# A hybrid decoder layer on one core: attention dealt in units of 128 keys, the first norm put ahead, the last tile cut in two

## The chip, the cores and the metric

The kernel runs on one core of one Trainium2 chip. The metric is device time in microseconds (us), the median of three runs. The engines are TensorE (PE: matrix products and transposes; its weight loads are listed apart as PEld), VectorE (DVE), ScalarE (ACT), GpSimd (POOL) and SyncE (SP, which issues most transfers). Each works through its own instructions in the order fixed when the program is built, and waits on semaphores for the others.

## The reference

One decoder layer over 512 tokens with 1024 channels, in float32:

```
u = rms_norm(x, norm_pre_mix);  proj = u @ w_in      # 9 projections
y_a = hgrn2_mixer(...)                               # gated recurrence, 8 heads
y_b = nsa_mixer(...)                                 # attention, 16 heads of 64, 4 groups of keys
merged = sigmoid(ga) * (y_a @ w_branch_a) + sigmoid(gb) * (y_b @ w_branch_b)
h = x + rms_norm(merged @ w_out, norm_post_mix)
v = rms_norm(h, norm_pre_mlp)
h = h + rms_norm(square(relu(v @ w_up)) @ w_down, norm_post_mlp)
e = (p @ w_ple) * sigmoid(h @ w_ple_gate)
out = h + rms_norm(e, norm_ple)
```

`nsa_mixer` has three branches for each head: softmax over 31 compressed keys, over selected blocks and over a window. With 512 tokens there are only 8 blocks of 64, all of them selected, and the window spans all earlier keys, so that the second and third branch are both full causal attention, each with keys and values of its own. Each branch is scaled by a gate and the three are added.

## The kernel before

Every product is made from three passes: each operand is split into a high part and a remainder, and high by high, high by remainder and remainder by high are added up in PSUM. A weight chunk is loaded by SP into `raw`; ACT casts it to `whi`, DVE subtracts for `wlo` (`pair_of`, `split`, lines 58 to 60 and 105 to 110). During attention the remainder is formed by ACT and an adding transfer from POOL's queue instead (`split_by_transfer`, lines 62 to 65).

**Start.** Token tile 0 is normed: ACT squares and sums, DVE and POOL form the factor, DVE writes `un` in two halves (L198), PE transposes them, ACT and DVE split the result into `uh` and `ul`. The first two weight chunks are cast and split on the same two engines at the same time.

**Attention** (`attend`) handles one group of four heads at a time, g = 0 to 3, over four query tiles t and two branches br: eight steps (t, br), each with t + 1 key tiles of 128. `scores` makes the scores of one step (PE, L474 and L476), their maxima (DVE, L478), the exponentials (ACT, L482), the scaling by gate and sum (DVE L492, ACT L495). `values` goes over the key tiles: PE transposes four heads (L162), ACT and DVE split them into `pth` and `ptl` (L59, L60), PE multiplies by V (L505, L506). Scores are made one step ahead. A generator yields after each step. So there are 20 key tiles in each group and 80 in all.

**The main stream** is the work that needs none of this: the projections for later groups (`kv_job`, `q_main`, each 96 products of 256 columns) and for the gates (`gate_tanh`, 24 products of 512 columns each). `mark` notes an instruction of attention with a weight, `rec` notes the first product of each threesome in the main stream, and `spread` then ties each of these, by an order-only dependency, behind the mark that lies in the same proportion. The order within an engine is otherwise made by a planner that takes what is ready by its own costs, earlier program text first. In the text before, whole steps of two groups are advanced (`advance`, lines 601 to 606), then a stretch of main stream is written, then `spread` is called; the transposes of queries and keys (`tr_r`, `q_rest`, `cmp_probs`) come in one lump for a group. Those transposes and the main stream share two PSUM banks (`mainp`, tag `main`). Keys and queries wait for their transposes in one tile, `stage`, with one buffer.

After attention come the recurrence (`hgrn_main`, `hgrn_head`), the two branch products, `w_out`, the MLP and the last product, `w_ple_gate`: two column halves by four token tiles, each half tile 24 products of 512 columns, then `evac_e` (lines 1179 to 1194): tanh, multiply, square with sum, the factor (`rms`), two final multiply-adds, two transfers by SP.

Of the kernel before, what the change touches and what calls it, by code (L numbers as in the profile page):

```python
# [7 lines left out]
FT = mybir.dt.float32  # L8
# [10 lines left out]
D = 1024  # L19
# [9 lines left out]
def hybrid_layer(ctx: ExitStack, tc: tile.TileContext, x, p, w_in, w_branch_a, w_branch_b, w_out,  # L29
# [40 lines left out]

    def mark(m, w=1.0):
        marks.append((m.ins, w + (marks[-1][1] if marks else 0.0)))
# [31 lines left out]

    def pair_of(src, a, b):
# [66 lines left out]
    with tc.tile_pool(name="pre", reuse_waits="tile", bufs=2) as pre, \  # L172
# [16 lines left out]
        for t in range(NT):  # L189
# [6 lines left out]
            for g in range(2):  # L196
                c = slice(g * 512, g * 512 + 512)
                dve.scalar_tensor_tensor(un[:, c], xs[t][:, c], rs, wps[:, c], op0=OP.mult, op1=OP.mult)  # L198
# [149 lines left out]
    def kv_job(pr, ck, cv, kdst, vdst, chunks=None):  # L348
        KH, KL, V = [], [], vdst
        st = ns.tile([128, 2, NT, 2, 128], FR, name="stage", bufs=1)  # L350
# [16 lines left out]
        for j in range(2):  # L367
            for src, dst, e in ((hn, KH, 0), (ln, KL, 1)):
                ps = tr_r([src[:, t, j] for t in range(NT)])
                kt = kdst[2 * j + e]  # L370
                if e:
                    act.copy(kt, ps.bitcast(FT))
                else:
                    dve.tensor_copy(kt, ps)
                dst.append(kt)
        return KH, KL, V

    def q_job(g):
        return q_rest(*q_main(g))

    def q_main(g):
        qsn = ns.tile([128, NT, 4, 128], FR, name="stage", bufs=1)
# [19 lines left out]
    def q_rest(qsn, qn):  # L402
        qs = [ns.tile([128, 512], FR, name="qs", tag="qs", bufs=8) for _ in range(4)]
# [6 lines left out]
        qt = []  # L410
# [8 lines left out]
        return qs, qt  # L419

    def cmp_soft(g, qt):
# [6 lines left out]
        sc = ns.tile([128, NT, 4, 32], FT, name="sc")  # L428
# [16 lines left out]
    def cmp_probs(sc):  # L445
        chl = []
# [10 lines left out]
        return chl  # L457

    def attend(g, qs, chl, kvs):
# [38 lines left out]
        def values(t, br, Ps, py):  # L498
            V = kvs[br][2]
            for kt in range(t + 1):  # L500
# [5 lines left out]
                mark(pe.matmul(py, V[j][:, kt], lo, start=False, stop=False), 1.0)  # L506

        def store(t, py):
# [27 lines left out]
    def together(*gens):  # L536
        live = list(gens)
        while live:
            live = [g for g in live if next(g, None) is not None]
# [8 lines left out]
    kv_dst = [kv_tiles(ns)]  # L548

# [4 lines left out]
    k0 = kv(0, 0, first_chunks)  # L554
# [24 lines left out]
    k1 = kv(0, 1)  # L579
    ph = cmp_core(0, kcd)  # L580
    q0, qt0 = q_job(0)
# [5 lines left out]
    c0 = cmp_probs(sc0)  # L587
# [13 lines left out]
    def advance(a, na, b=None, nb=0):  # L601
        for i in range(max(na, nb)):
            if i < na:
                next(a, None)
            if i < nb:
                next(b, None)

    a0 = attend(0, q0, c0, (k0, k1))
    advance(a0, 7)
    kb = kv(1, 0)  # L610
    gate_tanh(C_GB, gB_d, gp, 3, 4)
    q1 = q_main(1)
    spread(.9)
    marks.clear()
    rec.clear()
    gate_tanh(C_GB, gB_d, gp, 4, 5)
    q1, qt1 = q_rest(*q1)
    spread(1)
    c1 = cmp_probs(cmp_soft(1, qt1))
    spread(1)  # L620
    a1 = attend(1, q1, c1, (k0, k1))
    advance(a0, 3, a1, 6)
    kb = kb, kv(1, 1)
    q2 = q_main(2)
    spread(1)
    marks.clear()
    rec.clear()
    gate_tanh(C_GB, gB_d, gp, 5, 6)
    q2, qt2 = q_rest(*q2)
    spread(1)  # L630
    c2 = cmp_probs(cmp_soft(2, qt2))
    spread(1)
    a2 = attend(2, q2, c2, kb)
    advance(a1, 4, a2, 7)
    gate_tanh(C_GB, gB_d, gp, 6, 7)
    q3 = q_main(3)
    spread(.8)
    marks.clear()
    rec.clear()
    gate_tanh(C_GB, gB_d, gp, 7, 8)  # L640
    q3, qt3 = q_rest(*q3)
    spread(1)
    c3 = cmp_probs(cmp_soft(3, qt3))
    spread(1)
    a3 = attend(3, q3, c3, kb)
    advance(a2, 3, a3, 5)
    gate_tanh(C_GA, gA_d, gp, 0, 1)
    spread(1.1)
    advance(a3, 5)
    gate_tanh(C_GA, gA_d, gp, 1, 2)  # L650
    gate_tanh(C_GA, gA_d, gp, 2, 3)
    spread(1)
# [274 lines left out]
    def rows_of(ch, stat, nk, c, t, evac):  # L927
        ps = tp.tile([128, 512], FT, name="acc", tag="acc", bufs=3)
        s = slice(t * 128, t * 128 + 128)
        for k in range(nk):  # L930
            hi, lo = ch[k // 2]
            pe.matmul(ps, stat[0][:, k, s], hi[:, k % 2], start=(k == 0), stop=False)  # L932
            pe.matmul(ps, stat[0][:, k, s], lo[:, k % 2], start=False, stop=False)  # L933
            pe.matmul(ps, stat[1][:, k, s], hi[:, k % 2], start=False, stop=(k == nk - 1))  # L934
# [15 lines left out]
    def rms(pl, ss, eps):  # L950
        a = pl.tile([128, 1], FT, name="rsa")
        b = pl.tile([128, 1], FT, name="rsb")
        r = pl.tile([128, 1], FT, name="rsr")
        dve.tensor_scalar(a, ss[:, 0:1], 1.0 / D, eps, op0=OP.mult, op1=OP.add)
        dve.scalar_tensor_tensor(b, ss[:, 1:2], 1.0 / D, a, op0=OP.mult, op1=OP.add)
# [108 lines left out]
    def up_group(g):  # L1064
# [28 lines left out]
        if g == 1:  # L1093

            tc.add_manual_dep(m.ins, formed[-1].ins.name, mybir.DependencyInfo(
                mybir.DependencyClass.NoSync, mybir.DependencyReason.DATA), reason="forms first")
# [77 lines left out]
    sse = [ff.tile([128, 2], FT, name="sse", bufs=4) for _ in range(NT)]  # L1174
# [4 lines left out]
    def evac_e(c, t, ps):  # L1179
        tg = tgs[:, t % 2]  # L1180
        act.activation(tg, ps, AF.Tanh, scale=0.5)
        d = pw[:, t, c * 512:c * 512 + 512]
        dve.scalar_tensor_tensor(d, tg, 1.0, d, op0=OP.add, op1=OP.mult)
        sumsq(ff, d, sse[t][:, c:c + 1])
        z = rest[:, 2 * (t % 2) + c]
        if c == 0:
            z = d
        dve.tensor_mul(z, d, halves(w_pl)[c])
        if c == 1:
            r = rms(ff, sse[t], 4 * EPS)  # L1190
            for i, zz in enumerate((pw[:, t, 0:512], z)):
                o = rest[:, 2 * (t % 2) + i]
                dve.scalar_tensor_tensor(o, zz, r, halves(facc[:, t])[i], op0=OP.mult, op1=OP.add)
                sp.dma_start(out[t * 128:(t + 1) * 128, i * 512:i * 512 + 512], o)
    proj_n(w_ple_gate, (vh2, vl2), NK, evac_e)
# [57 lines left out]
```

## Time and profile before

| | us |
|---|---|
| median of 3 runs (lowest, highest) | 1234.18 (1232.11, 1237.09) |
| the profiled execution | 1235.09 |
| its span, first to last instruction | 1233.1 |
| PE busy in the span | 1191.1 |
| PE weight loads (overlapping) | 1039.4 |
| DVE busy | 781.4 |
| ACT busy | 641.3 |
| POOL busy | 146.8 |

The profiled execution lies 0.9 us above the median and 2.0 us above its own span. Busy time is the share of time in which an engine has an instruction in flight; since products are pipelined, a busy PE is not a PE at its best rate. The mean granted TensorE clock is 0.994 of full.

### The profile page before, as it was taken

The numbers are of one execution on the slowest core, as the hardware profiler recorded it, in microseconds if no ns is written. First come the engines' busy times: TensorE is split into PE (matmuls) and PEld (weight loads), VectorE is DVE, ScalarE is ACT, GpSimd is POOL, SyncE is SP. The second block draws the span as 40 slices with busy tenths as digits, with TensorE's granted clock in tenths as the row PEclk, the third lists the DMA queues.
The fourth block names the chain that finished last, engine by engine and source line by source line (L and its number), as shares of the span: only waits on it lengthen the run. The fifth ranks groups of instructions, "written<-read, shape, count | busy, mean of one in ns | idle before, by whom it ended". The sixth has DMA issues, their size and how long they took to land.

```text
span 1233.1 us, 18788 instructions
## 1 busy us (share of the span) xinstructions
PE 1191.1 (97%) x7159; PEld 1039.4 (84%) x7159; DVE 781.4 (63%) x1407; ACT 641.3 (52%) x1291; POOL 146.8 (12%) x282
## 2 busy tenths in 40 slices
PE   7999899999999999999999999999999999999997
PEld 6888797787878889898978788888989889889885
DVE  6774667737787366767675454588527457554664
ACT  6555878757886433434343322366637427336442
POOL 2020232221311110101010201000000000000000
PEclk9999999999999999999999999999999999999999
DMA  6337534242522432222223895434413324227401
GB/s 179 103 106 181 132 81 105 57 109 58 120 60 78 137 103 61 77 64 74 67 72 91 236 229 167 162 132 150 141 35 127 114 69 143 80 69 245 153 13 69
DMA packets 134188, 137.07 MB, mean 111 GB/s; under 512 B 8865, under 2 KB 108113, under 8 KB 134098
## 3 DMA queue, kind: packets, MB, share of 16 engines
q1 hardware_dynamic: 120352, 107.49, 30.0%
q0 software_dynamic: 5792, 19.93, 7.2%
q10 hardware_dynamic: 7954, 8.46, 2.1%
q8 instruction: 56, 0.92, 0.3%
q14 instruction: 34, 0.28, 0.1%
HBM read 111.73 MB, written 14.68 MB: 103 GB/s over the span
## 4 chain that ended last, share of the span: by engine, by line
PE 68%; DVE 2%; ACT 1%; DMA 1%; issue 0%; POOL 0%; ACTq 0%; DVEq 0%; POOLq 0%; SPq 0%
PE up L1054 11%; PE ps L86 6%; PE ps L87 6%; PE ps L88 5%; PE acc L1141 5%; PE acc L1140 5%; PE acc L1142 5%; PE lev L726 3%; PE acc L932 3%; PE acc L934 3%; PE acc L933 3%; PE ps L137 2%; PE ps L139 2%; PE ps L138 2%; PE tr L1054 2%; PE tr L162 1%
## 5 line engine op out<-in xcount | busy, mean ns | idle before, releaser
L59 ACT CAST whi<-raw 128x1024 fp32r<-128x1024 f32 (+1 forms) x181 | 188.4, 1046 | 215.3 <-PE acc L1142 59.1
L60 DVE TENSOR_TENSOR wlo<-raw,whi 128x1024 fp32r<-128x1024 f32 (+1 forms) x181 | 221.6, 1229 | 117.8 <-ACT whi L59 112.5
L137 PE MATMUL ps<-whi,uh 128*128 128x256 f32 (+1 forms) x512 | 147.4, 289 | 3.7 <-ACT gt L212 2.3
L138 PE MATMUL ps<-wlo,uh 128*128 128x256 f32 (+1 forms) x512 | 146.4, 286 | 0.2 <-DVE wlo L60 0.2
L139 PE MATMUL ps<-whi,ul 128*128 128x256 f32 (+1 forms) x512 | 146.3, 286 | 0.0
L86 PE MATMUL ps<-uh,whi 128*128 128x512 f32 x288 | 117.9, 409 | 0.2 <-DVE chl L456 0.2
L88 PE MATMUL ps<-uh,wlo 128*128 128x512 f32 x288 | 114.6, 398 | 0.3 <-DVE wlo L60 0.3
L87 PE MATMUL ps<-ul,whi 128*128 128x512 f32 x288 | 114.8, 399 | 0.0
L137 PEld LDWEIGHTS ps<-whi,uh 128*128 128x128 f32 x512 | 96.6, 189 | 6.8 <-ACT gt L212 2.9
L1141 PE MATMUL acc<-wlo,fh 128*128 128x512 f32 x256 | 101.2, 395 | 0.0
L1140 PE MATMUL acc<-whi,fh 128*128 128x512 f32 x256 | 100.5, 395 | 0.0
L1142 PE MATMUL acc<-whi,fl 128*128 128x512 f32 x256 | 99.9, 395 | 0.0
L138 PEld LDWEIGHTS ps<-wlo,uh 128*128 128x128 f32 x512 | 96.8, 189 | 1.2 <-DVE wlo L60 0.5
L139 PEld LDWEIGHTS ps<-whi,ul 128*128 128x128 f32 x512 | 96.7, 189 | 0.5 <-DVE ul L60 0.2
L482 ACT ACTIVATE P<-ps_s,nm 128x128 f32<-128x128 f32 (+3 forms) x128 | 67.7, 538 | 15.3 <-DVE nm L478 12.5
L478 DVE TENSOR_REDUCE nm<-ps_s 128x1 f32<-128x384 f32 (+3 forms) x88 | 55.7, 635 | 29.0 <-PE ps_s L476 28.5
L60 DVE TENSOR_TENSOR ptl<-tr,pth 128x512 fp32r<-128x512 f32 x82 | 55.6, 685 | 21.9 <-ACT pth L59 21.2
L88 PEld LDWEIGHTS ps<-uh,wlo 128*128 128x128 f32 x288 | 54.1, 188 | 12.5 <-DVE wlo L60 0.4
L474 PE MATMUL ps_s<-kt,qs 128*128 128x128 f32 (+3 forms) x256 | 60.4, 339 | 4.2 <-ACT P L482 3.7
L86 PEld LDWEIGHTS ps<-uh,whi 128*128 128x128 f32 x288 | 54.1, 188 | 11.1 <-PE py L532 0.6
L87 PEld LDWEIGHTS ps<-ul,whi 128*128 128x128 f32 x288 | 54.2, 188 | 10.3
L59 ACT CAST pth<-tr 128x512 fp32r<-128x512 f32 x82 | 47.7, 594 | 26.9 <-PE tr L162 25.9
(323 smaller groups left out, 2916.2 us busy)
## 6 DMA issues: line engine op xcount, KB each, us to landing
raw<-in_w_in_dram SPq DMA_DIRECT2D x58, 512.0 KB, 3.9
raw<-in_w_up_dram SPq DMA_DIRECT2D x32, 512.0 KB, 3.7
raw<-in_w_down_dram SPq DMA_DIRECT2D x32, 512.0 KB, 4.3
wlo<-raw POOLq DMA_DIRECT2D x18, 512.0 KB, 4.8
raw<-in_w_in_dram SPq DMA_DIRECT2D x17, 256.0 KB, 3.4
raw<-in_w_branch_a_dram SPq DMA_DIRECT2D x8, 512.0 KB, 8.6
raw<-in_w_branch_b_dram SPq DMA_DIRECT2D x32, 128.0 KB, 6.2
raw<-in_w_out_dram SPq DMA_DIRECT2D x8, 512.0 KB, 4.5
```

What stands on the lines that cost most here:

```text
L59: act.copy(hi, src)
L60: return dve.tensor_sub(lo, src, hi)
L86: rec.append(pe.matmul(ps, lh, rh, start=first, stop=False).ins)
L87: pe.matmul(ps, lh, rl, start=False, stop=False)
L88: pe.matmul(ps, ll, rh, start=False, stop=last)
L137: rec.append(pe.matmul(o, stat[0][:, k, s], hi[:, i], start=(k == 0), stop=False).ins)
L138: pe.matmul(o, stat[0][:, k, s], lo[:, i], start=False, stop=False)
L139: pe.matmul(o, stat[1][:, k, s], hi[:, i], start=False, stop=(k == NK - 1))
L1054: pe.matmul(ps[:, c], l[:, k, cs], r[:, k], start=f and n == 0, stop=e and n == 2, skip_group_check=True)
L1140: pe.matmul(ps, fh[:, k % 4, s], hi[:, k % 2], start=(k == 0), stop=False)
L1141: pe.matmul(ps, fh[:, k % 4, s], lo[:, k % 2], start=False, stop=False)
L1142: pe.matmul(ps, fl[:, k % 4, s], hi[:, k % 2], start=False, stop=(k == NK - 1))
```

## The change

- The low parts of the first weight chunks are ordered, on DVE, behind the second half of the norm of token tile 0 (`behind`, `lows`).
- `attend` yields after each key tile instead of after each step: a unit of 128 keys. `units` advances a group by n units and behind each takes one piece from another generator: `queries` (4 + 2 transposes of queries, the compressed scores, 4 transposes of probabilities) or `keys` (4 transposes of keys).
- The order of the stage is written anew. Each group has 20 units: nine, beside the next group's `q_main` (for the last group two gate tiles); then eleven, beside one gate tile and a `kv` job (groups 0 and 1) or two gate tiles (groups 2 and 3). `spread(1)` is called at each seam. The next group's first scores are written ahead of the last three units, except from group 1 to group 2, where they are written behind the last `kv` job and its key transposes. The number of products, transposes and gate tiles is the same.
- `stage` gets two buffers; `sc` has one instead of two; the tile `yl` is gone, its values are written over `ytmp`.
- At the end, the last token tile's second column half is computed as two pieces of 256 columns, with the sum of squares in three parts for that tile; in all four tiles the transfers of the second half are issued by ACT instead of SP.

The diff, cut to its core:

```
+    def behind(m, first, why):
+        tc.add_manual_dep(m.ins, first.ins.name, ... NoSync ..., reason=why)
...
-        w_split[0](hi, lo, src)
+        lows.append(w_split[0](hi, lo, src))
...
+                if t == 0 and g == 1:
+                    for low in lows:
+                        behind(low, m, "norm first")
...
-        st = ns.tile([128, 2, NT, 2, 128], FR, name="stage", bufs=1)
+        st = ns.tile([128, 2, NT, 2, 128], FR, name="stage", bufs=STAGES)    # 2
...
+        def keys():
+            for j in range(2):
+                for src, dst, e in ((hn, KH, 0), (ln, KL, 1)):
+                    ps = tr_r([src[:, t, j] for t in range(NT)])
...
+                    yield True
+        return (KH, KL, V), keys()
...
+    def queries(g, qm, qs, chl):
+        qt = []
+        yield from q_rest(*qm, qs, qt)
+        sc = cmp_soft(g, qt)
+        yield True
+        yield from cmp_probs(sc, chl)
...
-            yl = at.tile([128, 512], FR, name="yl", bufs=1)
+            yl = tmp.bitcast(FR)
...
-            values(t, br, pend, py)
+            units = values(t, br, pend, py)
             pend = nxt
-            if br:
-                pe.matmul(py, vch[:, t % 2, g], chl[t // 2], start=False, stop=True)
-                store(t, py)
-            yield True
+            for kt in range(t + 1):
+                next(units)
+                if br and kt == t:
+                    pe.matmul(py, vch[:, t % 2, g], chl[t // 2], start=False, stop=True)
+                    store(t, py)
+                yield True
...
+    def units(a, n, pieces=iter(())):
+        for _ in range(n):
+            next(a)
+            next(pieces, None)
+    a = attend(0, q0, c0, (k0, k1))
+    next(a)
+    left, kb = iter(()), []
+    for g in range(4):
+        units(a, 9, left)
+        whole(left)
+        if g < 3:
+            qm = q_main(g + 1)
+        else:
+            gate_tiles(2)
+        spread(1)
+        if g == 3:
+            units(a, 11)
+            gate_tiles(2)
+            spread(1)
+            break
+        qs, chl = [], []
+        pieces = queries(g + 1, qm, qs, chl)
+        units(a, 8, pieces)
+        kvs = (k0, k1) if g == 0 else kb
+        nxt = attend(g + 1, qs, chl, kvs)
+        if g != 1:
+            next(nxt)
+        units(a, 3, pieces)
+        whole(pieces)
+        gate_tiles(1 if g < 2 else 2)
+        if g < 2:
+            k, left = kv(1, g)
+            kb.append(k)
+        spread(1)
+        if g == 1:
+            whole(left)
+            next(nxt)
+        a = nxt
...
+            (act if o else sp).dma_start(out[t * 128:(t + 1) * 128, o:o + n], oo)
...
+            cuts = (0, 256, 512) if c and t == NT - 1 else (0, 512)
+            for n0, n1 in zip(cuts, cuts[1:]):
+                rows_of(ch, (vh2, vl2), NK, c, t, lambda ...: evac_e(c, t, ps, n0, n1), n0, n1)
```

## Rows read from the trace of the kernel before

**Rows 1.** The page: busy us, share of the span, instructions.

```profile
PE 1191.1 (97%) x7159; PEld 1039.4 (84%) x7159; DVE 781.4 (63%) x1407; ACT 641.3 (52%) x1291; POOL 146.8 (12%) x282
```

**Rows 2.** Windows: from:to, length, busy us by engine, granted clock, DMA share, GB/s.

```profile
133.00:410.00 277.00, 261.49 (x1656) 221.74 (x1655) 198.63 (x432) 208.14 (x527) 66.49 (x118) 0.99 0.36 84
240.00:265.00 25.00, 21.10 (x148) 18.69 (x145) 10.72 (x24) 15.08 (x33) 8.88 (x22) 0.93 0.48 104
277.00:291.00 14.00, 10.96 (x60) 8.21 (x59) 13.32 (x31) 10.56 (x28) 1.91 (x2) 0.88 0.40 95
291.00:324.00 33.00, 33.00 (x227) 30.16 (x225) 20.58 (x46) 26.16 (x66) 10.84 (x20) 1.00 0.31 68
324.00:360.00 36.00, 34.00 (x207) 27.35 (x205) 30.58 (x68) 30.40 (x81) 5.50 (x10) 1.00 0.42 100
```

**Rows 3.** PE's groups by shape, 133 to 410 us; first and last of 21.

```profile
L162 PE MATMUL tr<-ident,P 128*128 128x128 f32 x320 | 54.2, 280 | 2.8 <-DVE P L492 2.3 <-ACT P L495 0.3
...
L505 PE MATMUL py<-pth,V 128*128 128x512 f32 x80 | 34.6, 433 | 3.9 <-ACT pth L59 3.9
...
L476 PE MATMUL ps_s<-causal,identr 128*128 128x512 f32 x8 | 3.6, 444 | 0.0
```

**Rows 4.** The chain of waits: start, us on it, what (runs of one kind merged).

```profile
343.58 0.84 PE ps_s L474 x8
...
785.95 0.87 PE tr L162 x8
...
859.29 17.01 PE up L1054 x144
...
893.89 0.46 PE acc L1142 x2
```

**Rows 5.** Timeline of PE, 277 to 291 us: start, us, what.

```profile
283.48 0.28 PE L476 MATMUL ps_s<-causal,identr 128*128 128x256 f32 x1
285.13 1.16 PE L474 MATMUL ps_s<-kt,qs 128*128 128x256 f32 x4 [1.36 <-ACT P L482]
```

**Rows 6.** Waits of PE, 125 to 412 us: total us, times, longest.

```profile
PE ps_s L474 <- ACT P L482: 3.7, 8, 1.4
...
PE ps L137 <- ACT gt L212: 2.3, 2, 1.8
```

**Rows 7.** Timeline, a key job's last product and its last `stage` cast.

```profile
237.44 0.28 PE L139 MATMUL ps<-whi,ul 128*128 128x256 f32 x1
...
242.64 0.46 ACT L360 CAST stage<-knat 128x256 fp32r<-128x256 f32 x1
```

**Rows 8.** Timeline of the start: start, us, engine, what, idle before.

```profile
6.24 0.54 POOL L157 TENSOR_TENSOR rs<-ms,half 128x1 f32<-128x1 f32 x1 [4.29 <-DVE ms L156]
...
7.97 1.23 DVE L60 TENSOR_TENSOR wlo<-raw,whi 128x1024 fp32r<-128x1024 f32 x1 [1.81 <-ACT whi L59]
9.11 1.40 DVE L198 SCALAR_TENSOR_TENSOR un<-xt,rs,wps 128x512 f32<-128x512 f32 x2
...
11.06 0.59 ACT L59 CAST uh<-tr 128x512 fp32r<-128x512 f32 x1
```

**Rows 9.** Timeline of the end, behind PE's last product.

```profile
1224.51 0.60 ACT L1181 ACTIVATE tgs<-acc 128x512 f32<-128x512 f32 x1 [3.47 <-PE acc L934]
1225.13 0.69 DVE L1183 SCALAR_TENSOR_TENSOR pw<-tgs,pw 128x512 f32<-128x512 f32 x1 [1.77 <-ACT tgs L1181]
1225.86 0.63 ACT L948 ACTIVATE sqs<-pw 128x512 f32<-128x512 f32 x1 [0.76 <-DVE pw L1183]
...
1228.17 0.75 DVE L1193 SCALAR_TENSOR_TENSOR rest<-rest,rsr,facc 128x512 f32<-128x512 f32 x1
```

**Rows 10.** Groups by shape, 133 to 412 us: DVE and ACT on other widths.

```profile
L478 DVE TENSOR_REDUCE nm<-ps_s 128x1 f32<-128x512 f32 x32 | 21.9, 684 | 9.0 <-PE ps_s L476 8.9
L478 DVE TENSOR_REDUCE nm<-ps_s 128x1 f32<-128x384 f32 x32 | 17.5, 550 | 12.4 <-PE ps_s L476 12.2
L386 ACT ACTIVATE qn<-ps 128x256 f32<-128x256 f32 x12 | 4.6, 381 | 4.4 <-PE ps L139 4.4
```

More of the change, by code (lines that the diff above doesn't have):

```diff
@@ L366, in kv_job, with whole @@
               (uh, ul), mainp, evac)
[L367 to L379, printed above, removed]
+        def keys():
+            for j in range(2):
+                for src, dst, e in ((hn, KH, 0), (ln, KL, 1)):
+                    ps = tr_r([src[:, t, j] for t in range(NT)])
+                    kt = kdst[2 * j + e]
+                    if e:
+                        act.copy(kt, ps.bitcast(FT))
+                    else:
+                        dve.tensor_copy(kt, ps)
+                    dst.append(kt)
+                    yield True
+        return (KH, KL, V), keys()
+    def whole(*gens):
+        for gen in gens:
+            for _ in gen:
+                pass
     def q_main(g):
-        qsn = ns.tile([128, NT, 4, 128], FR, name="stage", bufs=1)
+        qsn = ns.tile([128, NT, 4, 128], FR, name="stage", bufs=STAGES)
         qn = ns.tile([128, NT, 256], FT, name="qn", bufs=1)
@@ L553, in hybrid_layer @@
     gp = tc.alloc_tile_pool(name="gp", reuse_waits="tile", bufs=2)
-    k0 = kv(0, 0, first_chunks)
+    k0, keys = kv(0, 0, first_chunks)
+    whole(keys)
     kcd = cmp_load(0)
@@ L578, in hybrid_layer @@
     vcd = cmp_load(1)
-    k1 = kv(0, 1)
+    k1, keys = kv(0, 1)
+    whole(keys)
     ph = cmp_core(0, kcd)
-    q0, qt0 = q_job(0)
+    q0, qt0, c0 = [], [], []
+    whole(q_rest(*q_main(0), q0, qt0))
     gate_tanh(C_GB, gB_d, gp, 0, 1)
@@ L599, in hybrid_layer @@
     rec.clear()
[L601 to L640, printed above, removed]
@@ L1173, in hybrid_layer @@
         sp.dma_start(pw[:, t], pw_d[t])
-    sse = [ff.tile([128, 2], FT, name="sse", bufs=4) for _ in range(NT)]
+    sse = [ff.tile([128, 3], FT, name="sse", bufs=4) for _ in range(NT)]
     down(3, evac_d3)
@@ L1177, in hybrid_layer, with evac_e @@
     tgs = ff.tile([128, 4, 512], FT, name="tgs", tag="fl")
-    def evac_e(c, t, ps):
-        tg = tgs[:, t % 2]
+    def evac_e(c, t, ps, n0=0, n1=512):
+        o = c * 512 + n0
+        tg = tgs[:, t % 2, n0:n1]
         act.activation(tg, ps, AF.Tanh, scale=0.5)
-        d = pw[:, t, c * 512:c * 512 + 512]
+        d = pw[:, t, o:o + n1 - n0]
         dve.scalar_tensor_tensor(d, tg, 1.0, d, op0=OP.add, op1=OP.mult)
[L1184 to L1195, printed above, removed]
+        piece = len(pieces[t])
+        act.activation(junk[:, :n1 - n0], d, AF.Square, accum_out=sse[t][:, piece:piece + 1])
+        z = d if c == 0 else rest[:, 2 * (t % 2) + 1, n0:n1]
+        dve.tensor_mul(z, d, w_pl[:, o:o + n1 - n0])
+        pieces[t].append((o, z))
+        if o + n1 - n0 < D:
+            return
+        r = rms(ff, sse[t], 4 * EPS, len(pieces[t]))
+        for o, zz in pieces[t]:
+            n = zz.shape[1]
+            oo = rest[:, 2 * (t % 2) + o // 512, o % 512:o % 512 + n]
+            dve.scalar_tensor_tensor(oo, zz, r, facc[:, t, o:o + n], op0=OP.mult, op1=OP.add)
+            (act if o else sp).dma_start(out[t * 128:(t + 1) * 128, o:o + n], oo)
+    junk = ff.tile([128, 512], FT, name="sqs", bufs=1)
+    pieces = [[] for _ in range(NT)]
+    for c in range(2):
+        ch = half_cols(w_ple_gate, NK, c)
+        for t in range(NT):
+            cuts = (0, 256, 512) if c and t == NT - 1 else (0, 512)
+            for n0, n1 in zip(cuts, cuts[1:]):
+                rows_of(ch, (vh2, vl2), NK, c, t,
+                        lambda c, t, ps, n0=n0, n1=n1: evac_e(c, t, ps, n0, n1), n0, n1)
     endp.release()
```

72 lines of the change are left out of this document (33 added, 39 removed).

## The prediction

> **What bounds the kernel now.** First the page's part on the engines: PE has something in flight for 1191.1 of 1233.1 us, 97% [rows 1]. No other engine comes near, so the time is PE's; the question is how much of it is work. Then windows by stretch: attention, 133 to 410 us, has PE busy for 261.5 of 277.0 us, so 15.5 us of visible idle time, more than a third of the 42 us in the whole span [rows 1, 2].
>
> Busy is not full rate, so I priced PE's work by its spacing. The chain of waits steps from product to product where nothing but PE holds it up: 17.01 us for 144 products of 256 columns is 0.118 us each, 0.46 for two of 512 is 0.23, 0.87 for eight float32 transposes is 0.109, 0.84 for eight of 128 columns is 0.105 [rows 4]. The listing by shape gives the counts of the stage, 21 rows [rows 3]: 504 products of 256 columns (59.5 us), 440 of 512 (101.2), 64 of 384 at 0.175, between the two (11.2), 392 transposes (42.7), 208 of 128 columns (21.8), 48 of 64 at no more than a transpose (5.2). Sum: 242 us. So the stage loses 277 - 242 = 35 us, 2.3 times the idle time that shows: around each visible wait PE also refills.
>
> By the Trainium skill (Perfetto Trace Analysis, Identifying the Most-Contended Engine) matmul busy time is no good measure and weight-load busy time is the better one. By that measure the stage's headroom would be 277 - 221.7 = 55 us, by busy time 15.5; the spacing lies between them, and I use the spacing.
>
> Where it is lost: the windows show two kinds of stretch. From 291 to 324 us the main stream flows between the steps: PE busy 33.0 of 33.0, with DVE at 62% and ACT at 79%. From 277 to 291 us no main stream is there: PE 10.96 of 14.0, DVE 95%. From 324 to 360 us, DVE 85% and ACT 84%, PE lacks 2.0 of 36 [rows 2]. The timeline shows what a bare stretch looks like: scores end at 283.8 us and the next wait 1.36 us for ACT's exponentials [rows 5]. In the list of waits it is the same names in small pieces, DVE and ACT steps of attention, longest 1.4 us [rows 6]. The granted clock is 0.93 and 0.88 in the two worst stretches, in which PE was idle for 3.9 and 3.0 us [rows 2]: for a part of them it was at the lower level, 1.2 GHz. In full-speed work that is 0.07 x 25 + 0.12 x 14 = 3.4 us lost, which is within the 35.
>
> **Attention, the sum.** No product, transpose, cast or transfer is added or removed in this stage; 242 us of PE work, 198.6 us of DVE, 208.1 of ACT stay [rows 2]. What changes is their mixture. Main stream: three `q_main` and two `kv` jobs at 96 x 0.118 = 11.3 us, eight gate tiles at 24 x 0.23 = 5.5: 101 us. Pieces: some 41 transposes of four and the compressed scores, about 14 us. The rest, 127 us, is 80 units: 1.6 us each, with 2.5 us of DVE and 2.6 of ACT (198.6/80, 208.1/80). A bare unit is therefore DVE- and ACT-bound, which is what 277 to 291 us shows; a unit with 1.25 us of main stream is PE's again, narrowly.
>
> The halves come out unequal. Nine units: 14.3 + 11.3 = 25.6 us of PE against 22.3 of DVE (87%) and 23.4 of ACT (91%): like the stretch from 324 to 360 us, whose idle share of 5.6% becomes a loss of 13% by the factor 2.3. Eleven units with their pieces: 17.6 + 4.7 + 16.8 = 39 us of PE against 27.3 and 28.6 (70%, 73%): nearest to 291 to 324 us, which shows no idle; I take 4%, since their chains of exponentials and casts stay. Four first halves: 13% of 102 = 13 us. The second halves hold the remaining 140 us: 4% is 6 us.
>
> One seam is new: from group 1 to group 2 the next scores stand behind the last `kv` job and its key transposes. In the trace the last `stage` cast of such a job starts 5.2 us after the job's last product [rows 7]. Two score steps can fill a part; 3 us, between 0 and 5.2. The other seams have their first scores three units ahead.
>
> Stage after: 242 + 13 + 6 + 3 = 264, so 13 us gained. The bounds: 30 if every stretch becomes like 291 to 324 us (242 + 5 for the refills); a loss of some 12 if the pieces stall PE (below).
>
> **Small edits there, priced at nothing.** `stage` with two buffers lets a query job write while keys are still transposed; the pieces behind units need it, and its own gain is in the 13. `yl` over `ytmp`: ACT's next write there now waits for the transfer of the remainder too, 2 to 3 us behind POOL, while stores lie at least two units, 6 us, apart; if POOL's queue, where adding transfers wait for ACT, is late by more, ACT stalls and the exponentials queue behind it. One `sc`: its next user comes a whole group later. Weight loads for the moved jobs go through the same SP and POOL queues, with DMA at 36% in the stage [rows 2].
>
> **Start.** The factor for tile 0 is ready at 6.78 us, but DVE begins `un` only at 9.11, behind the remainder of the first weight chunk (7.97, 1.23 us) [rows 8]. Reordered, `un` can begin up to 2.3 us earlier. But its transposes then want ACT, which is busy with the second weight chunk, and the remainders, now later, are themselves awaited by PE. I take 1.2 us, between 0 and 2.3. It reaches the end, as nothing but PE is behind it.
>
> **End.** After PE's last product come tanh 0.60, DVE 0.69, square 0.63, the factor, two multiply-adds of which the second starts at 1228.17, and a transfer [rows 9]. With 256 columns: ACT takes 0.38, and DVE, by the slope between 384 and 512 columns (0.134 us for 128), about 0.42 [rows 10]. So 0.2 + 0.3 + 0.2 saved; three final multiply-adds instead of two give 0.1 back; the last transfer is half as large and not behind SP's other one: 0.1. PE pays 48 x 0.118 - 24 x 0.23 = 0.1 more. Gain 0.6, between -0.5 and 1.5.
>
> A rule speaks against cutting products. The trace: 144 products of 256 columns, each with its own weight load, follow each other at 0.118 us [rows 4], though a load lasts 0.145 us on average (1039.4/7159) [rows 1]; so loads overlap. The Trainium skill (TensorE: Matmul & The Clock Gate, The mechanism) says that weight loads overlap products in flight only where their row groups differ, which is not so here. By that rule the 24 added loads would cost 3.5 us and the sum would be that much longer; by the row, nothing. The trace disagrees with the rule.
>
> **The sum** is made against the profiled execution's own 1235.09 us, 0.9 above the median of the runs: 1235.1 - 13 - 1.2 - 0.6 = 1220.3, which against the median is about 1220.
>
> **Rivals.**
> - *Everything flows* (1205): all units become like 291 to 324 us. Stage 250, gain 27; 1234.2 - 27 - 1.8. For it: PE was full there with ACT at 79%. Against it: DVE at 87% and ACT at 91% in the nine-unit halves.
> - *The order is new and the mixture is not good enough* (1231): the planner, not the text, makes the final order; if both halves lose 13%, as from 324 to 360 us, the stage is 242 + 31 + 3 = 276, gain 1. For it: in-order DVE and ACT serve attention, casts of weights and evacuations at once, and DVE is at 75% over the stage even when it lasts 264 us. Against it: the bare stretches, which lost most, are gone by construction.
> - *Two banks for pieces and main stream* (1245, slower): pieces used to come in lumps; now each takes one of the two `main` banks while a projection tile holds the other, so PE's next tile waits for a copy that stands behind exponentials on ACT. The nearest row is the main stream waiting for a gate tile's bank: 2.3 us in two times, longest 1.8 [rows 6]. At 0.6 us for each of 41 pieces it is 25 us: 1220 + 25. It makes the kernel slower than before from 0.36 us a piece, by over 0.5% from 0.5. Against it: pieces and tiles shared these banks before too, and only two such waits show.
>
> **How the numbers follow.** My forecast 55%, everything flows 14%, mixture not good enough 20%, banks 11%. A difference under 0.5%, 6 us, about what a measurement of this kernel can tell from none, puts the forecast and the first rival on the faster side (69%), the second within (20%), the third on the slower (11%). The forecast's own range is 1212 to 1228 (seam, 4 to 13% in the halves, start, end). The range of 8 in 10 reaches from 1206, leaving out the better half of the first rival, to 1239, leaving out the third.
>
> **What would show it.** Right: in the stage's windows PE idle falls from 15.5 us to about 8, with no stretch of 14 us under 90% busy; the clock row stays at 1.00; `un` starts near 6.9 us; from PE's last product to the last multiply-add 0.6 us less. Wrong: waits of PE's main stream (`ps`) on copies of `trr`, `pct` or `trq` tiles by the dozen; ACT's `ytmp` waiting for a transfer; an idle stretch of over 3 us where group 2 begins; the second remainder of the first weights awaited at the start.

## The result and the profile after

The change made the kernel slower. Its median is 1242.01 us (1239.39 to 1243.6, 8 runs) against 1233.69 (1232.01 to 1238.41, 8 runs) of the kernel before, a ratio of 1.006, 95% interval 1.0044 to 1.0077. Forecast were 1220 us with a range of 1206 to 1239; the median lies above it. The profiled execution took 1239.39 us, with a span of 1237.6. It is the fastest of the eight, 4.3 us above the profiled execution before where the medians differ by 8.3, so the two traces show about half of the loss.

The page's engines, answering [rows 1]: PE has 1.7 us more in flight in a span 4.5 us longer.

```profile
PE 1192.8 (96%) x7183; PEld 1043.1 (84%) x7183; DVE 778.6 (63%) x1411; ACT 644.5 (52%) x1294; POOL 144.9 (12%) x282
```

The milestones of the two traces say where. A product of the main stream at 50.7 us of before comes 1.2 us later, one at 669.8, well behind attention, 7.1 us later; one at 933.5 only 5.1, because before has the lower clock once more in between, at 842 us, in work that the change does not touch. The last tanh is 5.2 us later and the span 4.5. So in these traces attention loses about 6 us, the start about 1, and the end gives 0.7.

Windows of the kernel after, columns as in [rows 2]. First the whole stage, then the seam from group 1 to group 2:

```profile
131.00:417.00 286.00, 266.73 (x1679) 227.24 (x1677) 196.62 (x439) 212.44 (x534) 65.85 (x124) 0.98 0.35 82
...
280.00:294.00 14.00, 10.55 (x55) 9.76 (x55) 5.31 (x14) 8.08 (x24) 2.65 (x6) 0.63 0.70 151
```

PE lacks 19.3 us of the whole stage, 15.5 before. At the seam no engine is the bound: PE lacks 3.5 us, DVE is busy for 5.31 of 14, and the granted clock is 0.63. That is not the bare stretch of [rows 2], where DVE had 13.3 of 14. PE's timeline there (start, us, what, idle before and what ended it):

```profile
280.29 0.28 PE L146 MATMUL ps<-whi,ul 128*128 128x256 f32 x1
280.40 0.48 PE L354 MATMUL trr<-identr,stage 128*128 128x128 f32 x3
283.13 0.45 PE L354 MATMUL trr<-identr,stage 128*128 128x128 f32 x3 [2.25 <-DVE V L60]
284.37 0.83 PE L354 MATMUL trr<-identr,stage 128*128 128x128 f32 x2 [0.78 <-ACT stage L370]
285.52 0.75 PE L354 MATMUL trr<-identr,stage 128*128 128x128 f32 x4 [0.33 <-DVE kt L386]
286.06 1.40 PE L496 MATMUL ps_s<-kt,qs 128*128 128x128 f32 x5
...
289.98 0.42 PE L144 MATMUL ps<-whi,uh 128*128 128x256 f32 x1
290.20 0.42 PE L145 MATMUL ps<-wlo,uh 128*128 128x256 f32 x1
290.41 0.42 PE L146 MATMUL ps<-whi,ul 128*128 128x256 f32 x1
...
293.79 0.28 PE L144 MATMUL ps<-whi,uh 128*128 128x256 f32 x1
293.90 0.28 PE L145 MATMUL ps<-wlo,uh 128*128 128x256 f32 x1
```

The last product of the second `kv` job starts at 280.29 us. Its keys' transposes wait for the job's last evacuation (`V`) and casts (`stage`), the next scores wait for the transposes, and no unit is left to stand between. These scores are not group 2's first ones. The eight products of 128 columns and the mask of its first step, (0, 0), which needs only the keys of the earlier job, had run long before, although they are written behind the seam:

```profile
244.59 0.63 PE L496 MATMUL ps_s<-kt,qs 128*128 128x128 f32 x4
...
247.54 0.44 PE L498 MATMUL ps_s<-causal,identr 128*128 128x512 f32 x1
```

Group 2's first unit had run too (its last product starts at 260.21). What stands at the seam is the second step, (0, 1), which needs the keys of the job that has just ended. And although PE then runs again, products of 256 columns follow each other at 0.213 us instead of 0.118 until 293.8: the lower level, 1.2 GHz, granted after PE had idled.

The list of waits of PE over the stage (total us, times, longest), against [rows 6]:

```profile
PE ps_s L496 <- ACT P L504: 5.8, 14, 0.7
PE py L528 <- DVE ptl L60: 5.5, 7, 1.6
PE trr L354 <- DVE V L60: 2.3, 1, 2.3
...
PE ps L144 <- ACT gt L222: 0.7, 1, 0.7
```

The main stream's wait for a gate tile's bank has become shorter, and no waits on `trr`, `pct` or `trq` copies by the dozen are there. The main stream is nevertheless not dealt over the units. Windows over the half groups (nine units, then eleven, four times), instructions on the tile `ps`, the main stream, alone; the third column is PE:

```profile
130.00:159.70 29.70, 8.29 (x51) 7.25 (x51) 0.00 (x0) 1.17 (x3) 1.00 0.24 54
159.70:184.60 24.90, 0.00 (x0) 0.00 (x0) 0.00 (x0) 0.00 (x0) 1.00 0.32 78
184.60:225.80 41.20, 21.60 (x147) 19.66 (x148) 1.76 (x8) 3.37 (x14) 1.00 0.46 103
225.80:258.50 32.70, 8.29 (x69) 8.08 (x68) 0.00 (x0) 1.14 (x4) 1.00 0.33 73
258.50:320.60 62.10, 32.79 (x213) 30.12 (x214) 1.79 (x8) 4.09 (x16) 0.92 0.31 69
320.60:350.10 29.50, 0.52 (x3) 0.39 (x3) 0.00 (x0) 0.39 (x1) 0.94 0.37 81
```

Eleven units of group 0 pass with none of it, and eleven of group 2 with three products. What the text puts beside them comes in lumps behind the last piece of each group: the last probability transposes (`pct`) start at 187.5, 262.9 and 352.4 us, and the main stream, which had stopped at 156.3, 233.8 and 321.0, goes on at 189.8, 263.4 and 354.3.

The start, against [rows 8]:

```profile
6.81 1.41 DVE L205 SCALAR_TENSOR_TENSOR un<-xt,rs,wps 128x512 f32<-128x512 f32 x2 [0.66 <-POOL rs L164]
8.57 1.05 ACT L59 CAST whi<-raw 128x1024 fp32r<-128x1024 f32 x1 [0.72 <-DMA raw<-in_w_in_dram]
9.78 1.06 ACT L200 ACTIVATE sq<-xt 128x1024 f32<-128x1024 f32 x1 [0.17 <-DMA xt<-in_x_dram]
10.84 0.57 ACT L59 CAST uh<-tr 128x512 fp32r<-128x512 f32 x1
13.76 1.40 DVE L205 SCALAR_TENSOR_TENSOR un<-xt,rs,wps 128x512 f32<-128x512 f32 x2
```

`un` begins 2.3 us earlier, as forecast, but `uh`, on which the first product waits, only 0.2 us earlier (11.06 before): on ACT the second weight cast and the square of tile 1, which itself waits for its transfer, stand ahead. Tile 1's `un` moves from 12.38 to 13.76. In the lists of waits PE's wait for `un` at the start, before and after, has become shorter, and one for `uh` is new:

```profile
PE tr L162 <- DVE un L198: 3.3, 1, 3.3
```

```profile
PE ps L144 <- ACT uh L59: 2.4, 2, 1.9
...
PE tr L169 <- DVE un L205: 1.6, 1, 1.6
```

The end, against [rows 9]:

```profile
1229.19 0.28 PE L953 MATMUL acc<-whi,mgh 128*128 128x256 f32 x1
...
1229.31 0.28 PE L954 MATMUL acc<-wlo,mgh 128*128 128x256 f32 x1
1229.31 0.19 PEld L955 LDWEIGHTS acc<-whi,mgl 128*128 128x128 f32 x1
...
1229.43 0.28 PE L955 MATMUL acc<-whi,mgl 128*128 128x256 f32 x1
1229.74 0.38 ACT L1204 ACTIVATE tgs<-acc 128x256 f32<-128x256 f32 x1 [0.36 <-PE acc L955]
1230.16 0.42 DVE L1206 SCALAR_TENSOR_TENSOR pw<-tgs,pw 128x256 f32<-128x256 f32 x1 [0.59 <-ACT tgs L1204]
...
1232.71 0.87 DVE L1218 SCALAR_TENSOR_TENSOR rest<-rest,rsr,facc 128x256 f32<-128x256 f32 x2
```

From the last tanh's start to the end of the last multiply-add: 3.84 us, 4.41 before.

**A price for the stage.** With the prediction's own spacings, PE's work between 130 us and the stage's last unit can be counted and taken from its length. What is left is the loss, in us and good to about 1, here for some of the kernels below (nine-unit first halves, eleven-unit second halves; the order of before has no such halves):

| kernel | first halves | second halves | together |
|---|---|---|---|
| predicted, seam's 3 us in the first | 16 | 6 | 22 |
| before | | | 37.0 |
| after | 26.9 | 16.0 | 42.9 |
| seam mended, no norm order (e_seamnn) | 19.1 | 11.6 | 30.7 |
| own banks, seam mended (e_trseam) | 22.6 | 29.8 | 52.4 |
| the same, pieces spaced (e_flow) | 22.1 | 13.9 | 36.0 |
| e_seamnn, scores two ahead (e_two) | 16.0 | 11.2 | 27.2 |
| before, seam mended (e_bseam) | | | 35.2 |

### The profile page after: what moved, and what is told of

It reads as the page before. It is cut to its first block, busy times and chain, and to the rows that moved or that the text cites. A ratio compares the mean times of both kernels' runs of the same rounds, so it can differ in the third digit from the quotient of the medians.

```text
span 1237.6 us, 18868 instructions
## 1 busy us (share of the span) xinstructions
PE 1192.8 (96%) x7183; PEld 1043.1 (84%) x7183; DVE 778.6 (63%) x1411; ACT 644.5 (52%) x1294; POOL 144.9 (12%) x282
## 4 chain that ended last, share of the span: by engine, by line
PE 76%; ACT 3%; DVE 3%; DMA 2%; issue 2%; POOL 1%; SPq 0%; POOLq 0%; ACTq 0%; DVEq 0%
PE up L1076 11%; PE ps L91 6%; PE ps L92 6%; PE ps L93 6%; PE acc L1162 5%; PE acc L1161 5%; PE acc L1163 5%; PE ps L144 3%; PE ps L145 3%; PE ps L146 3%; PE lev L747 3%; PE acc L953 2%; PE acc L955 2%; PE acc L954 2%; PE tr L169 2%; PE ps_s L496 2%
## 5 line engine op out<-in xcount | busy, mean ns | idle before, releaser
L91 PEld LDWEIGHTS ps<-uh,whi 128*128 128x128 f32 x288 | 54.2, 188 | 12.2 <-PE ps_s L498 0.8
```

The source lines that it names most:

```text
L91: rec.append(pe.matmul(ps, lh, rh, start=first, stop=False).ins)
```

## The experiments

Each time is a median; the ratio is to runs of the kernel before on the same chip, whose medians were 1234.48, 1235.18, 1233.44 and 1233.09 us in the four sets of runs.

**Which part is it?** *e_noatt*: before with the norm order and the new end alone, attention untouched.

> The kernel before with the first and the last part of the change alone: the norm of tile 0 ahead of the low parts, and the last tile in two pieces with the transfers of the second halves from ACT; attention as before. If the attention part is what made the change slower, this is within 2 us of the kernel before (the start was 1.2 us later in the changed kernel's profile, the end 0.7 us shorter: 1234). If the start costs more than that (through the clock, which rose 1.7 us later), 1236 to 1238.

1234.43 us, ratio 0.9999 (0.9985 to 1.0013). The 8 us are attention's; start and end together give nothing that can be measured.

**The banks.** *e_tr*: the change with PSUM banks of their own for the pieces; *e_btr*: before with that edit alone.

```
-    trp[:] = [mainp, "main"]
     nsp = tc.alloc_tile_pool(name="nsp", ..., bufs=2, space=PSUM)
+    trp[:] = [nsp, "tr"]
```

> The changed kernel with one edit: the pieces (transposes of queries, keys and probabilities, and the compressed scores) take the two PSUM banks of attention's own transposes (tag tr) instead of the two main banks of the main stream. Theory of the banks: banks are handed out in the order in which tiles are written, so a main-stream tile written behind the pieces cannot start before the last piece has its bank, which is behind unit 18 to 21 of a group; with banks of their own for the pieces the gate tile and the kv job go beside units 10 to 20, the PE work between units 9 and 20 of groups 0 to 2 rises from 21 to 27 us to over 33, the loss over the stage falls by half and the time by 13 to 20 us, to 1222 to 1229, below the kernel before. Rival, the seam alone: the last kv job and its key transposes still stand right before group 2, so the wait and the low clock there stay and the time is 1237 to 1242. Rival, engines: DVE and ACT set the pace of a unit, dealing makes no difference, 1239 to 1243.

> The kernel before with the bank edit alone: its lumps of transposes take the banks of attention's own transposes. Theory of the banks: in the old order gate tiles are written ahead of the lumps and little of the main stream stands behind them, so the edit alone is worth little: within 5 us of before, 1229 to 1239. If the banks by themselves, without the new order, were the limit, 1215 to 1225.

e_tr: 1245.64 us, 1.0089 (1.0073 to 1.0105). e_btr: 1256.06, 1.0175 (1.016 to 1.019). Half of it held: the second halves now carry main stream (PE work behind the ninth unit of group 0: 37.4 us, 21.5 in the change), so the shared banks are what kept it out. That a bank is handed out in written order, so that the tiles written behind the pieces wait for the last one, fits where the main stream goes on in the change, 0.5 to 2.3 us behind the last `pct`. The time went the other way. The waits of PE in e_tr and, below, in e_btr name the cost:

```profile
PE pct L464 <- POOL sc L457: 7.2, 3, 2.8
...
PE trr L354 <- ACT stage L370: 4.1, 1, 4.1
```

```profile
PE pct L450 <- POOL sc L442: 14.4, 3, 5.3
```

With banks of their own the probability transposes stand in PE's order where the compressed softmax on DVE, ACT and POOL is not done, and everything behind them waits for it. In the change they come late enough: no such wait is in its list.

**The seam.** *e_seam*: both later `kv` jobs beside group 0, one gate tile to group 1, so that group 2's first scores too are written three units ahead. *e_lead*: those scores written ahead, but job and key transposes left at the seam. *e_keys*: the job moved, its key transposes (four groups of four) left at the seam, and with them the scores that need these keys.

```
-        if g != 1:
-            next(nxt)
+        next(nxt)                      # this edit alone: e_lead; e_keys leaves it out
...
-        gate_tiles(1 if g < 2 else 2)
-        if g < 2:
-            k, left = kv(1, g)
-            kb.append(k)
+        gate_tiles(2 if g else 0)
+        left = iter(())
+        if g == 0:                     # e_keys: the second `keys` is kept for the end of g == 1
+            for br in range(2):
+                k, keys = kv(1, br)
+                kb.append(k)
+                left = chain(left, keys)
...
-        if g == 1:                     # e_keys keeps this, e_lead only whole(left)
-            whole(left)
-            next(nxt)
```

> The changed kernel with one edit: both kv jobs are written beside group 0, the gate tile of group 0 goes to group 1, and the first scores of group 2 are written ahead like the others, so that no key transposes stand at the seam from group 1 to group 2. Pieces and main stream still share the two main banks. Theory of the seam: the 4.5 us of waits at 280 to 285 us and the 10 us at the lower clock (5 us lost) are gone: time down by 8 to 10 us, to 1232 to 1234. Theory of the banks: the same place is mended, but the units behind the ninth of each group stay bare (PE work between units 9 and 20 of groups 0 and 2 stays near 21 us of 25 to 30) and the main stream still comes in lumps behind them: down by 4 to 10 us, to 1232 to 1238, not below the kernel before. Engines: 1239 to 1243.

> The changed kernel with one edit: the first scores of group 2 are written ahead of the last three units of group 1, as at the other seams; the last kv job and its four key transposes stay at the seam, and the banks are shared as in the changed kernel. If the seam costs because PE has no scores to go on with, the wait of 4.5 us and the low clock shrink: 1231 to 1236. If it costs because the key transposes stand in PE's order right behind the kv job's last product and wait for its evacuation (2.3 us on VectorE's remainder of V, 0.8 on the stage cast), the wait stays: 1239 to 1243.

> As the change with the seam mended (both later kv jobs beside group 0, 1229.8), but the four key transposes of the second kv job stay where the change has them: at the seam from group 1 to group 2, ahead of group 2's first scores. The job itself is early, so its keys lie cast in their tile long before. It splits the seam's 12 us. If it is the transposes and copies of keys that stand between PE and group 2's first scores: 1238 to 1243. If it is the job that ends right at the seam, whose last evacuation and casts on ACT the transposes must wait for, then with the job early the four transposes run at once and it is 1229 to 1233.

e_seam: 1229.78 us, 0.9962 (0.9948 to 0.9977), 12 us below the change. e_lead: 1243.88, 1.0067 (1.0049 to 1.0085). This one decides nothing: its edit changed the text but not the order on PE. Up to 297 us its trace has the same sequence of products and transposes as the change, with the same scores of step (0, 0) far ahead of the seam:

```profile
246.22 0.63 PE L496 MATMUL ps_s<-kt,qs 128*128 128x128 f32 x4
```

e_keys: 1232.71, 0.9996 (0.9982 to 1.001). By the ratios 8 of the 12 us come with the job (1.006 - 0.9996) and 4 with its transposes and the scores behind them, each to about 2 us. PE's timeline of e_keys at its seam:

```profile
281.38 0.45 PE L355 MATMUL trr<-identr,stage 128*128 128x128 f32 x4
282.61 0.54 PE L355 MATMUL trr<-identr,stage 128*128 128x128 f32 x4 [0.78 <-DVE kt L387]
282.99 0.81 PE L497 MATMUL ps_s<-kt,qs 128*128 128x128 f32 x5
...
285.82 0.28 PE L145 MATMUL ps<-whi,uh 128*128 128x256 f32 x1
285.94 0.28 PE L146 MATMUL ps<-wlo,uh 128*128 128x256 f32 x1
```

The same 16 transposes and scores take 4.4 us (281.38 to 285.82), against 9.6 in the change (280.40 to 289.98), and the main stream goes on at 0.118: without the 2.25 us wait for the job's evacuation the clock stays at 2.4 GHz (granted clock 1.00 from 276 to 300 us).

**Even dealing with the seam mended.** *e_trseam*: e_seam with own banks. *e_flow*: the same, with query transposes two behind a unit and four units between the compressed scores and the first probability transposes. *e_spnn*: that spacing with shared banks and without the norm order.

```
-        yield from q_rest(*qm, qs, qt)
+        for n, _ in enumerate(q_rest(*qm, qs, qt)):
+            if n % 2:
+                yield True
         sc = cmp_soft(g, qt)
-        yield True
+        for _ in range(4):
+            yield True
```

> Both edits on the changed kernel: pieces in the banks of attention's own transposes, and both kv jobs beside group 0. The main stream stands beside nearly every unit in the order built. If uneven dealing was what cost, next to the seam, the stage loses at most 20 us and the time is 1214 to 1224. If the pieces' own chain costs (the probabilities' transposes stand close behind the compressed scores and wait for GpSimd's product, 7.2 us in three waits in the first bank experiment, and the clock falls behind them), it is 1228 to 1240, no better than with the seam edit alone (1230).

> The last one with a third edit: the transposes of queries come two behind a unit, and four units instead of one lie between the compressed scores and the first transposes of their probabilities. If the wait of these transposes for the softmax was what the bank edit cost, that wait is under 1 us and the time 6 to 14 us below the same kernel without this edit, 1212 to 1224. If ScalarE and VectorE set the pace of a unit (2.5 us each for 1.6 us of PE), it stays at 1227 to 1236.

> The change with the seam mended and without the norm order (1228.1), with query transposes two behind a unit and four units between compressed scores and first probability transposes, the banks still shared with the main stream. With own banks this spacing was worth 16 us. If it was worth that because the pieces' chain of softmax stood in PE's way, which in the kernel with shared banks shows no wait, it is worth nothing here: 1226 to 1230. If main tiles written behind the pieces get their bank only when the last piece is done, pieces that end later leave the middle of each group bare for no longer (the last piece stays where it is), and the same holds; if they end later, the main stream is squeezed and it is 1230 to 1236.

e_trseam: 1250.97 us, 1.0125 (1.0107 to 1.0143). e_flow: 1235.07, 0.9991 (0.9972 to 1.0009). e_spnn: 1227.26, 0.9949 (0.9932 to 0.9966), not told apart from e_seamnn below. PE's waits on the compressed softmax in e_trseam were

```profile
PE pct L465 <- POOL sc L458: 7.4, 3, 3.2
```

and none in e_flow. Windows of e_flow, tile `ps` alone, for the second halves of groups 0, 1 and 2:

```profile
163.20:207.20 44.00, 25.27 (x171) 21.66 (x172) 3.04 (x14) 4.20 (x21) 1.00 0.40 91
...
244.90:281.80 36.90, 12.24 (x45) 7.30 (x45) 0.00 (x0) 0.97 (x2) 1.00 0.38 91
...
313.60:352.50 38.90, 13.00 (x45) 7.43 (x46) 0.00 (x0) 1.01 (x2) 1.00 0.39 90
```

This is nearly the order that the prediction had taken from the text: main stream in every half group, and 1.5 us in all of PE waiting to transpose pieces. It took 1235 us, 4 to 5 more than e_seam with its bare second halves. So even dealing, with these banks, does not give the time back. Why it costs more is not settled: the pieces now share two banks with the units' own transposes, the stage loses 36.0 us against 31 to 32, and no single wait carries the difference. No run deals evenly without that sharing.

**The start.** *e_seamnn*: e_seam without the norm order; *e_nonorm*: the change without it.

```
-                if t == 0 and g == 1:
+                if False:
                     for low in lows:
                         behind(low, m, "norm first")
```

> The changed kernel with both kv jobs beside group 0 (1230) and without the order of the first norm ahead of the low parts. In the four profiles with that order the first job's last product comes 0.9 to 1.7 us later than in the two without it: without it 1228 to 1229.5. If the order helps or is nothing, 1230 to 1231.

> The change without its order-only dependency at the start (low parts of the first weights behind tile 0's norm), all else as it is. With the seam mended the same edit was worth 1.7 us in the medians, and the traces of all kernels with the norm order have the first kv job 0.9 to 1.7 us later. If that order costs what the traces show: 1240 to 1241 beside 1242.0. If the start is hidden in what follows: 1241.5 to 1242.5. If, as the prediction had it, the order gains 1.2 us: 1243 to 1244.

e_seamnn: 1228.08 us, 0.9936 (0.9915 to 0.9957). e_nonorm: 1242.41, 1.0069 (1.0042 to 1.0096), against 1242.01 of the change. The order gains nothing. At the start the traces agree: from the start of its first to that of its last product, the first job takes 18.5 us in all eight traces with that order and 17.0 to 17.3 in the nine without it (in e_two below, without it, the job ends 0.9 us late because it begins 1.0 us late). Whether these 1.2 to 1.5 us reach the end, the medians do not settle: 1.7 us in one pair, none in the other.

**What the new order is worth.** *e_bseam*: before, its steps of two groups kept, with both later `kv` jobs in the first stretch and a gate tile moved in return.

```
-    kb = kv(1, 0)
-    gate_tanh(C_GB, gB_d, gp, 3, 4)
+    kb = kv(1, 0), kv(1, 1)
...
-    kb = kb, kv(1, 1)
+    gate_tanh(C_GB, gB_d, gp, 3, 4)
```

> The kernel before, its old order of whole steps kept, with the second kv job of the later key groups written beside group 0 with the first one, and the gate tile that stood there moved to group 1: the seam edit alone, without any other part of the change. It asks what the new order of units is worth when both orders have the seam mended. If the new order is worth the 13 us that the prediction gave it, the mended old order stays well above the mended new one without the norm (1228.1): 1233 to 1240. If the order is worth little and the seam is what moved the time, the old order gains as well: 1225 to 1231. If the old order had no trouble at its seam, the extra kv job beside group 0 only makes the stretch behind it barer: 1236 to 1242, with PE's windows between 180 and 290 us losing more.

1232.58 us, 0.9989 (0.997 to 1.0008). The old order has no such trouble to mend; the seam is the change's own. Against e_seamnn's 1228.08 the new order with a mended seam is worth 4.5 us by the medians, 6.5 by the ratios, the new end included.

**Short steps.** *e_two*: e_seamnn with scores two steps ahead in each group's three shortest steps, their exponentials packed into fewer tiles (not shown below); *e_flowtwo*: the same on e_flow, without the norm order; *e_sptwo*: on e_spnn.

```
-        pend = scores(*steps[0])
+        pend, made = [scores(*s) for s in steps[:2]], 2
...
-            nxt = scores(*steps[i + 1]) if i + 1 < len(steps) else None
+            upto = min(len(steps), i + (3 if i < 3 else 2))
+            while made < upto:
+                pend.append(scores(*steps[made]))
+                made += 1
```

> The change with the seam mended and without the norm order (1228.1), and scores made two steps ahead instead of one for the three shortest steps of each group (their exponentials packed into fewer tiles, so that no memory is added). In that kernel the four first halves (nine units each) lose 5.8, 3.6, 6.9 and 2.8 us, 19 together, against 13 predicted. Latency theory: short steps have too little PE work to cover scores, maxima, exponentials and scaling one step ahead; with two ahead the loss falls by a third to a half, 6 to 9 us: 1219 to 1222. Throughput theory (DVE 86% and ACT 90% busy in the first nine units, as the prediction reasoned): nothing to gain, 1226 to 1231, and the exponentials of later steps put ahead of casts that PE waits for could make it slower.

> As the run before it, but with banks of the pieces' own, query transposes two behind a unit and four units between compressed scores and the first probability transposes (that kernel with the norm order and one step ahead took 1235.1, without the norm order some 1233.5). Here the main stream is dealt evenly and the pieces wait for nothing. Latency theory: it gains like the run before it, 6 to 9 us: 1225 to 1228. Throughput theory: 1231 to 1236.

> All edits that helped, together: seam mended, no norm order, scores two steps ahead in the three shortest steps, query transposes two behind a unit and four units between compressed scores and first probability transposes; banks shared as in the change. If the gains add: 1228.1 less 3.9 (two ahead) less 0.8 (spacing), 1223 to 1224. If PE is by now short of nothing but what the granted clock takes, no better than two ahead alone: 1224 to 1227.

e_two: 1224.15 us, 0.9935 (0.9913 to 0.9956). e_flowtwo: 1227.56, 0.9956 (0.994 to 0.9972), 7.5 below e_flow by the medians and 4 by the ratios, of which the norm order can be 1 to 2. e_sptwo: 1225.2, 0.9935 (0.9912 to 0.9957). How much two steps ahead are worth is not settled: e_two is 3.9 us below e_seamnn by the medians and equal to it by the ratios; against e_spnn, measured on the same chip, it is 2 to 3 us lower. The first halves lose 16.0 us instead of 19.1 (in a profiled execution of 1231.06, the longest of its eight). That suggests, without showing it, that a part of what the prediction laid to DVE's and ACT's load is the latency of the short steps' chain. The gains do not add; e_two and e_sptwo are 8 to 9 us below before and 15 to 18 below the change, and beat both.

## Why the prediction was wrong

**What bounds the kernel** held: PE sets the time, and the loss of the stage counted by spacing follows the times to about 2 us. From the change to e_seamnn the loss falls by 12.2 us and the time by 13.9; from before to e_seamnn by 6.3 and 7.1, of which 0.6 are the end.

**The seam failed**, "3 us, between 0 and 5.2": the step took [rows 7]'s 5.2 us from last product to last cast as the whole price and let two score steps fill a part. Mending it gave 12 us back. Nothing fills it: group 1's units, group 2's first scores and its first unit are used up before the job ends, and the next scores need the job's own keys. What PE does then runs at the lower clock. 3.4 us of idle time are listed, but the stretch from 280.40 to 289.98 is 5.1 us longer than the same work in e_keys, and the products up to 293.79 lose another 18 x (0.213 - 0.118) = 1.7. These 6.8 us are most of the 8 between e_keys and the change. The place of the transposes and their scores, the other 4, is only partly seen: the eleven units behind them, whose window has 0.94 of the clock (320.6 to 350.1 us), lose 6.9 us in the change, 5.4 in e_keys and 3.9 in e_seamnn.

**The mixture failed**, "13 us gained": it stood on every unit having main stream beside it "by construction". The text says so, the trace does not: with two banks shared with the pieces, the main stream comes in lumps behind them. The size was wrong too. e_flow, where the dealing is even, is within the forecast's 4% in one second half (1.2 us of 44.0) but shows 16 to 17% in two others (6.1 of 36.9, 6.2 of 38.9). In e_seamnn first halves lose 19.1 against 13 priced, second halves 11.6 against 6: together 12 us above their price, which with the 9 us that the seam cost above its 3 is about the 22 us by which the forecast was missed. The division into units had a slip that changes little: it took off 101 us for five whole jobs and the gate tiles, but the 242 us hold 424 of the jobs' 480 products (504 less the scores' 80), so a unit has 1.7 us of PE and not 1.6. What the new order is worth, 4.5 to 6.5 us where 16 had been forecast without the seam, is e_seamnn against e_bseam.

**The start failed**, "1.2 us, between 0 and 2.3": DVE's part came as forecast, `un` at 6.81, but the step's own caveat decided. ACT reached `uh` only 0.2 us earlier, tile 1's `un` comes 1.4 us later, PE waits 2.4 us for `uh` where before lists no such wait, and the first job takes 1.2 to 1.5 us longer in every trace that has the order.

**The end held**: 0.57 us to the last multiply-add, 0.7 with the transfer, 0.6 forecast. It does not show in the times: e_noatt, which has the start and the end, is level with before. Products of 256 columns follow each other at 0.12 us there (1229.19, 1229.31, 1229.43), though each has its own load of 0.19. The Trainium skill (TensorE: Matmul & The Clock Gate, The mechanism), in its list of what overlaps, would have loads overlap only where row groups differ; this trace disagrees again.

**The rivals.** The one on the slower side gave the right size, 1245, by the wrong road: it wanted some 41 waits of 0.6 us of the main stream for copies of pieces, and the list has one of 0.3; the longest wait of the main stream for a bank is 0.7, on a gate tile's evacuation. Two banks do matter, but in another way: they keep the main stream out of the middle of each group, and giving the pieces banks of their own made it worse until their chain was spaced. "Everything flows" is not borne out: e_flow, where the main stream flows in every half group, took 1235. "Mixture not good enough", 1231, is near what the order does once its seam is mended (1229.8). "An idle stretch of over 3 us where group 2 begins" had been named as a sign of error; it came in three pieces, 3.4 us together and the longest 2.25.

**Not shown**: which of ACT's and DVE's steps sets the remaining loss of the first halves; why own banks with spaced pieces stay 4 to 5 us above shared ones; and what scores two steps ahead gain.

## What to carry to other kernels

Price a seam by what PE has to do between the last product of the job and the first work that needs it: when that is nothing, it costs the whole chain of evacuation, cast, transpose and copy, and then some more at the lower clock; put the job a group earlier instead. Read in the trace, not in the text, what stands at the seam: here the planner had put the first scores ahead by itself, and e_lead's edit changed nothing there. Text that deals work evenly deals nothing if the work takes its buffers in written order from a pool that the other stream also uses: look for the main stream's tile in windows over the units before believing it. And a buffer that is removed as a bottleneck may have been holding work back until its inputs were ready.

## What the runs showed of the hardware

The price of a short idle time is not the idle time. After gaps of 2.25, 0.78 and 0.33 us, PE's products went at 0.213 instead of 0.118 us for as long as the row of the timeline shows, up to 293.8 us, when it had had work again for 8 us; e_keys, with gaps of 0.78 us and less at the same place, kept the full clock.
